# Reciprocal square roots of the norms on VectorE instead of GpSimd, and one set of SBUF offsets for both feed-forward blocks

## The chip, the core and the metric

The kernel runs on one core of one Trainium2 chip. The metric is device time in microseconds (us) of one execution, taken as the median of several runs of the same program. The engines are PE (TensorE), DVE (VectorE), ACT (ScalarE), POOL (GpSimd) and SP (SyncE, which here only starts DMAs).

## The reference

Two transformer blocks run one after the other on 256 tokens of width 1024. The first has a mixer (mLSTM and sliding-window attention), a cross attention to a memory, and a PEER layer over 16384 experts. The second has an even mixer (stick-breaking attention and retention), a convolutional feed-forward layer (`ffn0`), an odd mixer (gated linear attention) and a second feed-forward layer (`ffn1`). Each of these layers begins with a root-mean-square norm, and the first block ends with one:

```python
def rms_norm(x, g):
    xf = x.astype(jnp.float32)
    y = xf * lax.rsqrt(jnp.mean(xf * xf, axis=-1, keepdims=True) + EPS)
    return (y * g.astype(jnp.float32)).astype(x.dtype)

def conv_ffn(hn, w_up, conv_w, conv_b, w_down):
    u, v = jnp.split(hn @ w_up, 2, axis=-1)
    up = jnp.pad(u, ((0, 0), (CONV_WIDTH - 1, 0), (0, 0)))
    uc = conv_b + conv_w[0] * up[:, 0:s]
    for j in range(1, CONV_WIDTH):
        uc = uc + conv_w[j] * up[:, j:j + s]
    return (jax.nn.silu(uc) * v) @ w_down
```

Inside the even and odd mixers the same norm is also taken per head (of q, k and of the outputs).

## The kernel before

The activation `h` lies in SBUF with the 1024 features on 128 partitions in 8 tiles of 256 tokens. Every large product is made of three matmuls in a reduced float format: the operand is split into a high and a low part, and hi*hi, hi*lo and lo*hi are added up in PSUM. For weights, `weight` reads a piece of 512 KB over SP into `raw`; ACT writes `hi` (L430), DVE subtracts it and writes `lo` (L431). Five sets of raw, hi and lo buffers rotate up to the PEER layer and six after it, so a new piece can be split only when PE has done with an older one. L440 to L442 and L582 to L584 are the three matmuls, of 256 or 512 columns.

`Norm` splits the unnormalized `h` times the gain into `xh` and `xl` and lets the projection start on them; the reciprocal root is applied when the projection's result is taken from PSUM. It is made meanwhile: ACT and DVE square and add, PE sums over the partitions with a matmul against a column of ones (L200), `rsqrt` (L451 to L474) works on a tile of 128x2, and `spread` (L213 and L215) turns it into a row, `xR` or `uR`, by two matmuls against an identity and an ACT copy. Evacuations that need the row are queued until it is there. In program order the root is written after the first piece of the projection, the row after the third.

`rsqrt` has twelve operations: `rs_m` on DVE (L454) and eleven on POOL (a first guess from the bits, a refined `rs_z`, one more step to `rs_y` at L473). The chain stands alone: each operation needs the one before. `Final`, the norm between the two blocks, does two such roots in a row with three small products on POOL between and behind (L297, L298, L300), since it applies two norms at once. `head_norm` (L1349 to L1355) does the roots per head, with `rs_m` on POOL as well. `ev_o` in the mixer of the first block makes a negated copy `nr` on POOL.

The order in which instructions stand on each engine is not the order of the code. A scheduler lays them out by its own costs and by the buffers and pieces of work that are free; each engine then runs its list strictly in order.

Places in SBUF come from pools, in the order in which the pools are opened. `skip` (L397) takes some bytes and so moves all that follows in its pool; `off` moves a norm's tiles within their slot (`placed`). Before, the norm of `ffn1` has `off=16` elements and `ffn1` skips 32 bytes, where the other norms have 0 and `ffn0` skips 96. In the built program `xh` and `xl` begin at bytes 191552 and 199872 of a partition for the norms of even, ffn0 and odd, and at 191616 and 199936 for ffn1; `uh` and `ul`, the feed-forward layer's operands of the down product, begin at 119872 and 126016 in ffn0 and at 119808 and 125952 in ffn1.

## Time and profile before

| what | us |
|---|---|
| median of three runs | 1731.04 |
| lowest and highest of them | 1727.76 and 1736.29 |
| the profiled execution, its own time | 1739.33 |
| its span, first to last instruction | 1737.6 |
| PE busy in the span | 1683.0 |
| DVE, ACT, POOL busy | 1241.1, 873.8, 89.1 |

The profiled execution was 8.3 us above the median. A wait in the view of waits is time in which an engine had nothing to run, put down to what ended it. A row of the timeline is one instruction (or several alike): its start, its length, the engine, the line, what it writes and reads, and in brackets how long the engine was idle before it and what released it. [...] Matmuls overlap in the pipeline, so one is shown as longer than the distance between the starts of two.

### The profile page before, as it was taken

What the parts mean: (1) busy time and instruction counts of PE and PEld (TensorE: products, weight loads), DVE (VectorE), ACT (ScalarE), POOL (GpSimd) and SP (SyncE); (2) the same over time, 40 slices, a digit from 0 to 9 for tenths busy, and PEclk for the clock granted to TensorE, in tenths of its full rate; (3) what the DMA queues carried; (4) which work ended last, traced back from release to release, by engine and by line L of the source; (5) the groups of instructions that cost most, each with busy time, mean ns of one, the idle gap of its engine ahead of it and who ended that gap; (6) DMA issues with size and microseconds to landing.
All of it is one profiled execution on the core that took longest, in us unless ns stands there. A gap on an engine that the chain in (4) does not pass through costs nothing.

```text
span 1737.6 us, 33082 instructions
## 1 busy us (share of the span) xinstructions
PE 1683.0 (97%) x13220; PEld 1602.0 (92%) x13220; DVE 1241.1 (71%) x2309; ACT 873.8 (50%) x1358; POOL 89.1 (5%) x246
## 2 busy tenths in 40 slices
PE   7999999999999999999999999899999999999999
PEld 6879889999999999989999999678999987799998
DVE  6686559998798985678555556686777765677775
ACT  6445345545455554444444446464555454455543
POOL 1011010000000000000000000401100010210000
PEclk9999999999999999999999999999999999999999
DMA  7434454577555655889655556443455544345551
GB/s 263 152 104 147 146 172 131 187 236 260 175 186 199 194 196 188 309 289 299 190 189 186 185 189 210 157 135 110 162 192 186 191 159 155 102 162 190 188 188 62
DMA packets 97516, 318.03 MB, mean 183 GB/s; under 512 B 11841, under 2 KB 13505, under 8 KB 96850
## 3 DMA queue, kind: packets, MB, share of 16 engines
q1 hardware_dynamic: 89154, 301.39, 53.1%
q10 hardware_dynamic: 8208, 14.52, 2.2%
q8 instruction: 104, 1.70, 0.4%
q14 instruction: 50, 0.41, 0.1%
HBM read 299.36 MB, written 16.52 MB: 182 GB/s over the span
## 4 chain that ended last, share of the span: by engine, by line
PE 70%; DVE 7%; DMA 3%; POOL 2%; issue 2%; ACT 1%; SPq 0%; POOLq 0%; DVEq 0%; ACTq 0%
PE tp L440 11%; PE tp L441 11%; PE tp L442 11%; PE acc L582 8%; PE acc L583 8%; PE acc L584 8%; PE acc L440 3%; PE acc L441 3%; DMA u<-store 3%; PE acc L442 3%; DVE lo L431 2%; PE tp L1192 1%; PE tp L1193 1%; DVE ga L1244 1%; DVE w L1345 1%
## 5 line engine op out<-in xcount | busy, mean ns | idle before, releaser
L430 ACT ACTIVATE hi<-raw 128x1024 fp32r<-128x1024 f32 (+1 forms) x533 | 560.2, 1057 | 660.8 <-PE tp L441 246.6
L431 DVE TENSOR_TENSOR lo<-raw,hi 128x1024 fp32r<-128x1024 f32 (+1 forms) x533 | 646.7, 1219 | 309.5 <-ACT hi L430 309.2
L440 PE MATMUL tp<-xh,hi 128*128 128x256 f32 x1680 | 476.7, 284 | 0.6 <-ACT u L1207 0.6
L441 PE MATMUL tp<-xl,hi 128*128 128x256 f32 x1680 | 471.8, 281 | 0.0
L442 PE MATMUL tp<-xh,lo 128*128 128x256 f32 x1680 | 471.1, 280 | 0.6 <-DVE lo L431 0.6
L442 PEld LDWEIGHTS tp<-xh,lo 128*128 128x128 f32 x1680 | 317.1, 189 | 0.8 <-DVE lo L431 0.8
L440 PEld LDWEIGHTS tp<-xh,hi 128*128 128x128 f32 x1680 | 317.0, 189 | 0.8 <-ACT u L1207 0.8
L441 PEld LDWEIGHTS tp<-xl,hi 128*128 128x128 f32 x1680 | 317.2, 189 | 0.0
L583 PE MATMUL acc<-u,hi 128*128 128x256 f32 x1024 | 288.4, 282 | 5.6 <-DVE u L436 5.6
L584 PE MATMUL acc<-u,lo 128*128 128x256 f32 x1024 | 288.2, 281 | 1.4 <-DVE lo L431 1.4
L582 PE MATMUL acc<-u,hi 128*128 128x256 f32 x1024 | 287.9, 281 | 0.0
L583 PEld LDWEIGHTS acc<-u,hi 128*128 128x128 f32 x1024 | 193.0, 188 | 6.4 <-DVE u L436 6.4
L584 PEld LDWEIGHTS acc<-u,lo 128*128 128x128 f32 x1024 | 196.9, 192 | 1.8 <-DVE lo L431 1.8
L582 PEld LDWEIGHTS acc<-u,hi 128*128 128x128 f32 x1024 | 193.0, 189 | 0.0
L440 PE MATMUL acc<-hi,xh 128*128 128x512 f32 (+1 forms) x256 | 103.5, 406 | 1.6 <-ACT y L479 1.6
L441 PE MATMUL acc<-lo,xh 128*128 128x512 f32 (+1 forms) x256 | 101.7, 397 | 0.5 <-DVE lo L431 0.5
L442 PE MATMUL acc<-hi,xl 128*128 128x512 f32 (+1 forms) x256 | 101.1, 395 | 0.0
L582 PE MATMUL acc<-uh,hi 128*128 128x256 f32 x352 | 98.3, 280 | 0.1
L583 PE MATMUL acc<-ul,hi 128*128 128x256 f32 x352 | 98.1, 279 | 0.0
L584 PE MATMUL acc<-uh,lo 128*128 128x256 f32 x352 | 98.1, 279 | 0.0
L457 POOL TENSOR_SCALAR rs_g<-rs_m 128x2 int32<-128x2 int32 (+2 forms) x20 | 10.2, 510 | 1263.8 <-DVE fq L296 810.3
L582 PE MATMUL acc<-oh,hi 128*128 128x256 f32 x256 | 73.1, 285 | 0.0
(436 smaller groups left out, 2801.8 us busy)
## 6 DMA issues: line engine op xcount, KB each, us to landing
raw<-down SPq DMA_DIRECT2D x128, 512.0 KB, 3.7
raw<-up SPq DMA_DIRECT2D x128, 512.0 KB, 4.4
raw<-ffn_up SPq DMA_DIRECT2D x88, 512.0 KB, 3.5
raw<-ffn_down SPq DMA_DIRECT2D x44, 512.0 KB, 3.4
raw<-even_in SPq DMA_DIRECT2D x28, 512.0 KB, 4.4
store<-u ACTq DMA_DIRECT2D x55, 256.0 KB, 3.4
u<-store SPq DMA_DIRECT2D x55, 256.0 KB, 4.7
raw<-odd_in SPq DMA_DIRECT2D x24, 512.0 KB, 3.5
```

The source lines that it names most:

```text
L430: nc.scalar.activation(hi[:, c], raw[:, c], AF.Copy)
L431: nc.vector.tensor_sub(lo[:, c], raw[:, c], hi[:, c].bitcast(F32))
L440: mm(out, lh, rh, start=start, stop=False)
L441: mm(out, lh, rl, start=False, stop=False)
L442: mm(out, ll, rh, start=False, stop=stop)
L582: mm(out, wh[:, cs], oh, start=start and j == 0, stop=False)
L583: mm(out, wh[:, cs], ol, start=False, stop=False)
L584: mm(out, wl[:, cs], oh, start=False, stop=stop and j == 1)
L1192: mm(o, p1[:, b, :, e], hi[:, b, :, e], start=True, stop=False)
L1193: mm(o, p1[:, b, :, e], lo[:, b, :, e], start=False, stop=True)
L1244: nc.vector.tensor_mul(src, src, a)
L1345: nc.vector.match_replace(out=w, in_to_replace=val[:, :8], in_values=s, imm_value=-3e38)
```

## The change

All of `rsqrt` runs on DVE, in ten operations: a multiplication and an addition, or two multiplications, are fused into one (`scalar_tensor_tensor`) at three places. `Final`'s small products and `nr` run on DVE too. POOL keeps nothing of the roots. Behind the norms, `off` is 0 everywhere and both feed-forward layers skip 96 bytes. The tile `rs_b` falls away; the new pool `gaps` takes its 64 bytes.

```diff
-        nc.vector.tensor_copy(q, ps[:, 2:4])
-        nc.gpsimd.tensor_mul(q, q, self.rf)
-        nc.gpsimd.tensor_mul(q, q, self.rf)
-        r = b.rsqrt(q, 2, 1.0, keep=self.tag, e=nc.gpsimd)
-        nc.gpsimd.tensor_mul(r, r, self.rf)
+        nc.vector.tensor_mul(q, ps[:, 2:4], self.rf)
+        nc.vector.tensor_mul(q, q, self.rf)
+        r = b.rsqrt(q, 2, 1.0, keep=self.tag)
+        nc.vector.tensor_mul(r, r, self.rf)
...
-        e = self.nc.gpsimd
-        e.tensor_scalar(gi, ms.bitcast(I32), -0.5, float(0x5F1FFFF9), op0=ALU.mult, op1=ALU.add)
+        v.tensor_scalar(gi, ms.bitcast(I32), -0.5, float(0x5F1FFFF9), op0=ALU.mult, op1=ALU.add)
-        e.tensor_mul(a, y, y)
-        e.tensor_mul(a, a, ms)
-        e.tensor_scalar(a, a, -0.703952253, 0.703952253 * 2.38924456, op0=ALU.mult, op1=ALU.add)
+        v.tensor_mul(a, y, y)
+        v.scalar_tensor_tensor(a, a, -0.703952253, ms, op0=ALU.mult, op1=ALU.mult)
-        e.tensor_mul(z, y, a)
-        a = sp.tile([P, n], F32, tag="rs_b", name="rs_b")
-        e.tensor_mul(a, z, z)
-        e.tensor_mul(a, a, ms)
+        v.scalar_tensor_tensor(z, a, 0.703952253 * 2.38924456, y, op0=ALU.add, op1=ALU.mult)
+        v.tensor_mul(a, z, z)
+        v.tensor_mul(a, a, ms)
-        e.tensor_scalar(p, a, 0.375, -1.25, op0=ALU.mult, op1=ALU.add)
-        e.tensor_mul(p, p, a)
-        e.tensor_scalar(p, p, 1.875, None, op0=ALU.add)
+        v.scalar_tensor_tensor(p, a, -10.0 / 3.0, a, op0=ALU.add, op1=ALU.mult)
+        v.tensor_scalar(p, p, 0.375, 1.875, op0=ALU.mult, op1=ALU.add)
-        e.tensor_mul(out, p, z)
+        v.tensor_mul(out, p, z)
...
-            return lambda: Norm(self, self.h, i, self.xq, off=16 if i == 8 else 0)
+            return lambda: Norm(self, self.h, i, self.xq, off=0)
...
+            self.skip(self.pool(ctx, "gaps"), 64)
...
-                nc.gpsimd.tensor_scalar(nr, x.r[t], -1.0, None, op0=ALU.mult)
+                nc.vector.tensor_scalar(nr, x.r[t], -1.0, None, op0=ALU.mult)
...
-            self.skip(mp, 32 if l else 96)
+            self.skip(mp, 96)
```

In the built program the ten operations do not stand together. On DVE around the norm of ffn0 there stood before, with `lo` the low half of a weight piece, `rs_m` the first operation of the root and `w` the first evacuation that needs `xR`:

```order
L454 TENSOR_SCALAR rs_m_14523<-tp_14520 128x2
L431 TENSOR_TENSOR lo_14634<-raw_14631,hi_14633 128x1024
L431 TENSOR_TENSOR lo_14673<-raw_14670,hi_14672 128x1024
L431 TENSOR_TENSOR lo_14713<-raw_14710,hi_14712 128x1024
L431 TENSOR_TENSOR lo_14747<-raw_14744,hi_14746 128x1024
L431 TENSOR_TENSOR lo_14778<-raw_14775,hi_14777 128x1024
L1538 TENSOR_TENSOR w_14612<-acc_14495,xR_14607 128x256
```

On the same engine at the same place there stands now (lines of the changed file; its `lo` is L430):

```order
L453 TENSOR_SCALAR rs_m_14488<-tp_14485 128x2
L430 TENSOR_TENSOR lo_14596<-raw_14593,hi_14595 128x1024
L455 TENSOR_SCALAR rs_g_14490<-rs_m_14488 128x2
L430 TENSOR_TENSOR lo_14635<-raw_14632,hi_14634 128x1024
L458 TENSOR_TENSOR rs_a_14492<-rs_g_14490 128x2
L430 TENSOR_TENSOR lo_14675<-raw_14672,hi_14674 128x1024
L459 SCALAR_TENSOR_TENSOR rs_a_14492<-rs_a_14492,rs_m_14488 128x2
L430 TENSOR_TENSOR lo_14709<-raw_14706,hi_14708 128x1024
L461 SCALAR_TENSOR_TENSOR rs_z_14495<-rs_a_14492,rs_g_14490 128x2
L430 TENSOR_TENSOR lo_14740<-raw_14737,hi_14739 128x1024
L462 TENSOR_TENSOR rs_a_14492<-rs_z_14495 128x2
L430 TENSOR_TENSOR lo_14780<-raw_14777,hi_14779 128x1024
```

Each step of the root is now followed by a `lo`, six in all, of which the sixth stood behind `w` before; the last four steps follow without one.

On PE around the row of the odd mixer's norm there stood before, with `xR`'s matmul at L213 between the last product of one weight piece and the first of the next:

```order
L441 MATMUL acc_16944<-lo_16966,xh_16758 128x512
L442 MATMUL acc_16944<-hi_16965,xl_16759 128x512
L213 MATMUL tp_16982<-ident_87,rs_y_16941 128x128 x2
L440 MATMUL acc_16943<-hi_16997,xh_16758 128x512
L441 MATMUL acc_16943<-lo_16998,xh_16758 128x512
```

On PE there stands at that place now:

```order
L439 MATMUL acc_16903<-hi_16956,xh_16720 128x512
L440 MATMUL acc_16903<-lo_16957,xh_16720 128x512
L213 MATMUL tp_16941<-ident_92,rs_y_16900 128x128 x2
L441 MATMUL acc_16903<-hi_16956,xl_16721 128x512
L439 MATMUL acc_16902<-hi_16978,xh_16720 128x512
```

L213 moved behind eleven of the next piece's twelve matmuls. In the same way it moved behind 21 matmuls of 128x256 in the first mixer, 22 in the cross attention, and behind 13 of those and five smaller ones in the PEER queries; in the memory's norm, the even mixer and both feed-forward layers it stayed.

On DVE in `Final` of the even mixer there stood before, with the rest of both roots on POOL and `y` the evacuation that waits for them:

```order
L454 TENSOR_SCALAR rs_m<-tp 128x2
L296 COPY fq<-tp 128x2
L431 TENSOR_TENSOR lo<-raw,hi 128x1024 x4
L481 TENSOR_SCALAR y<-acc,rs_y 128x512
L431 TENSOR_TENSOR lo<-raw,hi 128x1024
```

On DVE there stands now, from the end of the first root (ahead of it eight `lo` stand between its steps):

```order
L468 TENSOR_TENSOR rs_y_13176<-rs_p_13173,rs_z_13169 128x2
L296 TENSOR_TENSOR fq_13178<-tp_13157,rs_y_13176 128x2
L297 TENSOR_TENSOR fq_13178<-fq_13178,rs_y_13176 128x2
L453 TENSOR_SCALAR rs_m_13181<-fq_13178 128x2
L455 TENSOR_SCALAR rs_g_13183<-rs_m_13181 128x2
L430 TENSOR_TENSOR lo_13506<-raw_13503,hi_13505 128x1024
L458 TENSOR_TENSOR rs_a_13185<-rs_g_13183 128x2
L307 SCALAR_TENSOR_TENSOR h_8918<-h_8918,g_89,fR_13336 128x256
L459 SCALAR_TENSOR_TENSOR rs_a_13185<-rs_a_13185,rs_m_13181 128x2
```

All eight residual operations `h` (L307), which stood much later before, now stand between the second root's steps, so `y` stands behind nine `lo` and eight `h`.

Of the offsets, in the built program all norms from even on have `xh` at 191808 and `xl` at 200000, and ffn1 has `uh` and `ul` where ffn0 has them. The weight buffers keep their addresses.

## Rows read from the trace of the kernel before

**Rows 1.** The page's first part: busy us, share of the span, instructions.

```profile
PE 1683.0 (97%) x13220; PEld 1602.0 (92%) x13220; DVE 1241.1 (71%) x2309; ACT 873.8 (50%) x1358; POOL 89.1 (5%) x246
```

**Rows 2.** Waits of PE: what it waited for, us in total, times, longest.

```profile
PE tp L213 <- POOL rs_y L473: 19.3, 7, 3.3
...
PE tp L1383 <- DVE y L1377: 5.9, 2, 5.4
...
PE tp L599 <- DVE ro L1503: 2.7, 1, 2.7
```

**Rows 3.** Timeline of PE at the norm of ffn0.

```profile
1231.10 0.28 PE L442 MATMUL acc<-xh,lo 128*128 128x256 f32 x1
1234.22 0.71 PE L213 MATMUL tp<-ident,rs_y 128*128 128x128 f32 x4 [2.85 <-POOL rs_y L473]
```

**Rows 4.** Timeline of POOL at the same place: fifth and sixth of eleven operations.

```profile
1231.42 1.05 POOL L464 TENSOR_TENSOR rs_z<-rs_g,rs_a 128x2 f32<-128x2 f32 x1
1232.55 0.19 POOL L466 TENSOR_TENSOR rs_b<-rs_z 128x2 f32<-128x2 f32 x1
```

**Rows 5.** Timeline of DVE at the same place.

```profile
1226.59 0.15 DVE L454 TENSOR_SCALAR rs_m<-tp 128x2 f32<-128x2 f32 x1
1226.66 5.75 DVE L431 TENSOR_TENSOR lo<-raw,hi 128x1024 fp32r<-128x1024 f32 x5
```

**Rows 6.** Timeline of ACT at the same place: the sixth weight piece.

```profile
1231.30 1.06 ACT L430 ACTIVATE hi<-raw 128x1024 fp32r<-128x1024 f32 x1 [1.25 <-DVE lo L431]
```

**Rows 7.** Timeline of DVE in the first mixer: two small operations, the second needing the first.

```profile
81.01 0.17 DVE L880 TENSOR_TENSOR ss<-ss,rc 128x8 f32<-128x8 f32 x1
81.21 0.17 DVE L881 TENSOR_TENSOR ss<-ss,rc 128x8 f32<-128x8 f32 x1
```

**Rows 8.** Windows after two waits of PE: length, busy us by engine, PEclk, DMA share, GB/s.

```profile
105.70:109.10 3.40, 3.29 (x21) 2.46 (x22) 2.17 (x8) 2.09 (x7) 0.00 (x0) 1.00 0.58 223
...
1234.80:1238.20 3.40, 3.40 (x19) 3.40 (x18) 2.81 (x6) 1.48 (x3) 0.00 (x0) 0.50 0.64 251
```

**Rows 9.** Timeline of PE at the norm of the odd mixer.

```profile
1421.47 0.40 PE L441 MATMUL acc<-lo,xh 128*128 128x512 f32 x1
1421.71 0.40 PE L442 MATMUL acc<-hi,xl 128*128 128x512 f32 x1
1425.02 0.71 PE L213 MATMUL tp<-ident,rs_y 128*128 128x128 f32 x4 [2.91 <-POOL rs_y L473]
```

**Rows 10.** Timeline of PE at the memory's norm.

```profile
105.74 0.71 PE L213 MATMUL tp<-ident,rs_y 128*128 128x128 f32 x4 [1.19 <-POOL rs_y L473]
```

**Rows 11.** Timeline of PE in the even mixer, at `Final`.

```profile
1097.53 0.51 PE L440 MATMUL acc<-hi,xh 128*128 128x512 f32 x1 [1.62 <-ACT y L479]
...
1105.99 1.11 PE L1383 MATMUL tp<-ident,y 128*128 128x128 f32 x4 [5.40 <-DVE y L1377]
```

**Rows 12.** Timeline of DVE at the same place.

```profile
1085.81 0.16 DVE L454 TENSOR_SCALAR rs_m<-tp 128x2 f32<-128x2 f32 x1 [1.14 <-PE tp L200]
```

**Rows 13.** Instructions of line 308: engine, operation, count, ns (least, median, most).

```profile
L308 DVE SCALAR_TENSOR_TENSOR h<-h,g,fR x8: 470/477/478, 1113.6 to 1130.4; 128x256 f32<-128x256 f32 x8
```

**Rows 14.** Timeline of DVE at the output norm of the retention.

```profile
1196.83 0.67 DVE L1354 TENSOR_REDUCE rn1s<-rn1q 128x4 f32<-128x512 f32 x1
1198.34 1.23 DVE L431 TENSOR_TENSOR lo<-raw,hi 128x1024 fp32r<-128x1024 f32 x1 [0.84 <-ACT hi L430]
1202.48 1.14 DVE L1503 SCALAR_TENSOR_TENSOR ro<-ro,rs_y,gate 128x128 f32<-128x128 f32 x4 [2.92 <-POOL rs_y L473]
```

**Rows 15.** Windows in the PEER layer, in ffn0 and in ffn1; first busy us and count: PE.

```profile
789.00:801.00 12.00, 12.00 (x109) 12.00 (x108) 9.60 (x12) 5.59 (x7) 0.00 (x0) 1.00 0.96 325
809.00:1071.00 262.00, 262.00 (x2227) 262.00 (x2226) 145.60 (x150) 121.38 (x140) 0.00 (x0) 1.00 0.62 197
1240.00:1405.00 165.00, 164.87 (x1417) 164.68 (x1417) 121.80 (x185) 85.37 (x123) 0.00 (x0) 1.00 0.57 186
1560.00:1725.00 165.00, 165.00 (x1401) 165.00 (x1400) 117.69 (x178) 81.17 (x117) 0.00 (x0) 1.00 0.50 162
```

More of the change, by code (lines that the diff above doesn't have):

```diff
@@ L449, in copy, with rsqrt @@
             self.nc.vector.tensor_copy(out, in_)
-    def rsqrt(self, ss, n, inv, keep=None, e=None):
-        sp = self.sp
+    def rsqrt(self, ss, n, inv, keep=None):
+        sp, v = self.sp, self.nc.vector
         ms = sp.tile([P, n], F32, tag="rs_m", name="rs_m")
-        (e or self.nc.vector).tensor_scalar(ms, ss, inv, EPS, op0=ALU.mult, op1=ALU.add)
-        e = self.nc.gpsimd
+        v.tensor_scalar(ms, ss, inv, EPS, op0=ALU.mult, op1=ALU.add)
         gi = sp.tile([P, n], I32, tag="rs_g", name="rs_g")
-        e.tensor_scalar(gi, ms.bitcast(I32), -0.5, float(0x5F1FFFF9), op0=ALU.mult, op1=ALU.add)
+        v.tensor_scalar(gi, ms.bitcast(I32), -0.5, float(0x5F1FFFF9), op0=ALU.mult, op1=ALU.add)
         y = gi.bitcast(F32)
         a = sp.tile([P, n], F32, tag="rs_a", name="rs_a")
-        e.tensor_mul(a, y, y)
-        e.tensor_mul(a, a, ms)
-        e.tensor_scalar(a, a, -0.703952253, 0.703952253 * 2.38924456, op0=ALU.mult, op1=ALU.add)
+        v.tensor_mul(a, y, y)
+        v.scalar_tensor_tensor(a, a, -0.703952253, ms, op0=ALU.mult, op1=ALU.mult)
         z = sp.tile([P, n], F32, tag="rs_z", name="rs_z")
-        e.tensor_mul(z, y, a)
-        a = sp.tile([P, n], F32, tag="rs_b", name="rs_b")
-        e.tensor_mul(a, z, z)
-        e.tensor_mul(a, a, ms)
+        v.scalar_tensor_tensor(z, a, 0.703952253 * 2.38924456, y, op0=ALU.add, op1=ALU.mult)
+        v.tensor_mul(a, z, z)
+        v.tensor_mul(a, a, ms)
         p = sp.tile([P, n], F32, tag="rs_p", name="rs_p")
-        e.tensor_scalar(p, a, 0.375, -1.25, op0=ALU.mult, op1=ALU.add)
-        e.tensor_mul(p, p, a)
-        e.tensor_scalar(p, p, 1.875, None, op0=ALU.add)
+        v.scalar_tensor_tensor(p, a, -10.0 / 3.0, a, op0=ALU.add, op1=ALU.mult)
+        v.tensor_scalar(p, p, 0.375, 1.875, op0=ALU.mult, op1=ALU.add)
         out = sp.tile([P, n], F32, tag="rk_" + keep if keep else "rs_y", name="rs_y")
-        e.tensor_mul(out, p, z)
+        v.tensor_mul(out, p, z)
         return out
@@ L1354, in head_norm @@
         nc.vector.tensor_reduce(ss, sq, axis=AX.X, op=ALU.add)
-        return self.rsqrt(ss, n, 1.0 / d, keep=tag, e=nc.gpsimd)
+        return self.rsqrt(ss, n, 1.0 / d, keep=tag)
     def even(self, x, nxt):
```

## The prediction

> **What bounds the kernel now.** The page's first part comes first: PE is busy 97% of the span, DVE 71%, POOL 5% [rows 1]. What PE loses is 1737.6 - 1683.0 = 54.6 us of idle time and whatever it runs at a lower clock. Second, the view of waits says for what PE stood idle: 19.3 us, in seven waits, for POOL's last step of a root (`rs_y`) at L213 [rows 2]. Third, one of them is read in the timelines, at ffn0. PE starts its last free matmul at 1231.10 and goes on at 1234.22 with the matmul that spreads the root [rows 3]. On POOL the fifth step of the chain takes 1.05 us and the sixth 0.19 us [rows 4], though they are alike in size. What changed between them is DVE: it ran five `lo` in a row from 1226.66 to 1232.41 [rows 5]. So the chain is slow because a POOL step beside a `lo` takes as long as that `lo`, about 5.75/5 = 1.15 us; alone, eleven steps of 0.19 us would be 2.1 us of work.
>
> Fourth, the clock. In the 3.4 us after ffn0's wait of 2.85 us PEclk is 0.50; after the memory's wait of 1.19 us it stays 1.00 [rows 8, 10]. A stretch of 3.4 us at half clock does the work of 1.7, so a wait near 3 us costs 1.7 us more than its length.
>
> **The chain on DVE, step by step.** It is not put on a free engine: between its steps the order has a `lo` each, and DVE runs them strictly in order. In a queue a small operation takes its place in 1226.66 - 1226.59 = 0.07 us [rows 5]; where it needs the one before, 81.21 - 81.01 = 0.20 us [rows 7]. At ffn0 that is six `lo` of 1.15 us and six small steps among them, then four dependent steps. From 1226.59 the first five `lo` and six small steps end at 1226.59 + 5.75 + 6 x 0.07 = 1232.8; the sixth `lo` has its `hi` from 1232.36 [rows 6] and ends at 1233.9; four steps of 0.20 bring `rs_y` to 1234.7. L213 stood at 1234.22 with POOL; it is not moved there, so PE waits **0.6 us longer**, between 0 and +1.4 (all steps at 0.20). ffn1 is built alike: 1.2 us together, bounds 0 and 2.8.
>
> Where the gain comes from is PE's own order. At **four norms** (first mixer, cross attention, PEER queries, odd mixer) L213 now stands behind more matmuls. That is 21 or 22 of 128x256 at 165/1417 = 0.116 us [rows 15], or 2.5 us; eleven of 128x512 at 1421.71 - 1421.47 = 0.24 us [rows 9], or 2.6 us; in the PEER queries 13 and five smaller ones, some 2.0 us if the small ones are priced alike. The mean is 2.4 us. The chain itself is as long as before, since five or six `lo` stand in it on either engine, so the wait of (19.3 - 1.2)/6 = 3.0 us [rows 2, 10] falls to 0.6. With more work done ahead, PE comes sooner to a PSUM bank that only the queued evacuations free; this costs between nothing and one more length of L213's group, 0.71 us [rows 3]; no row shows it, and I take 0.3, nearer to nothing since L213's own length is only part of that way. Saved: 4 x (2.4 - 0.3) = **8.4 us**, bounds 6.7 and 9.6.
>
> The **memory's norm** keeps L213's place, and its chain now has `lo`s and two other evacuations between. Its wait of 1.19 us [rows 10] becomes 2.5 by the same count as at ffn0, with one more `lo` than there beside POOL: +1.3, bounds 0 and +3.
>
> **Final** gets longer. From `rs_m` at 1085.81 [rows 12]: eight `lo`, 9.2 us, ten steps of which four dependent, 0.6 + 0.8; `fq` and the next two, 0.8; a ninth `lo`, 1.15; eight residuals of 0.48 [rows 13] less the overlap of 0.07, 3.3; the steps among and behind them, 1.0: `y` starts at 1102.6. PE's next matmul followed `y` by some 0.7 us at 1097.53 [rows 11]; it moves to 1103.3, 5.8 later. But twelve matmuls on, PE waited once more, until 1105.99, for the q heads' norm [rows 11], two roots on POOL. At the **retention** two such roots take from the end of the last sum, 1197.50, to 1202.48 for the first [rows 14], 5.0 us; on DVE the two stand in pairs, 20 steps of 0.07 to 0.20, 1.4 to 4.0 us, of which I take 2.0 (ten dependent distances, the partner in their shadow), plus the `lo` at 1198.34, 1.15 or more. So `ro` starts 1.5 us sooner there and the wait of 2.7 us [rows 2] falls to 1.2: **-1.5**, bounds 0 and -2.7. At the q heads the pair saves 3.0 and the `lo` that stood among them 0.8 more: 5.8 - 3.8 = **+2.0**, bounds 0 and +5.8.
>
> The other roots (k heads, odd outputs) and `nr` have no wait in rows 2 and lie beside PE's matmuls: nothing. If that cover were gone, each would cost its chain of 2.0 us.
>
> Waits together: -8.4 - 1.5 + 1.2 + 1.3 + 2.0 = **-5.4 us**.
>
> **The clock.** Five waits (the four and the retention's) fall below 1.2 us, and after one of 1.19 PEclk stayed at 1.00 [rows 8]. Each gives 1.7 us back; as one of the four may meet a second wait at the PSUM bank just behind, I count four: **-6.8**, bounds -8.5 and 0. Of the memory's 2.5 us no row tells; it lies between 1.19 and 2.85, and I count nothing and keep +1.7 as a bound. Both ffn and the even mixer keep their half-clock stretches.
>
> **The offsets.** In equal stretches PE ran 1417 matmuls in ffn0 and 1401 in ffn1 [rows 15]: 0.1164 against 0.1178 us each. ffn1 gets ffn0's offsets for `uh` and `ul`, and the same `xh` and `xl`. If the pace hangs on these, its some 180 us at 1.1% give **-2.0**. But PEER speaks against a pace by offsets alone: on one set of buffers it had 109 matmuls in 12 us (three of them begun before, so 0.113 each) and then 2227 in 262 us, 0.1177 [rows 15]. So both layers could settle at 0.113, -4.9 and -7.1 (1540 matmuls each), or both at 0.1178, +2.1 and 0. I take -2.0, the pace that the same operands have in ffn0; bounds -12.0 and +2.1. [...]
>
> **Sum.** -5.4 - 6.8 - 2.0 = -14.2 us. The profiled execution would take 1739.3 - 14.2 = 1725.1. It was itself 8.3 above the median of the runs, so against that the forecast is 1731.0 - 14.2 = **1716.8 us**.
>
> **The rivals.**
> A: both feed-forward layers settle at 0.113: ten more, 1707. For it: PEER's first stretch and the rest of the offsets being equal; against: it lasted only 12 us there.
> B: half the clock and no offsets: -5.4 - 3.4 = -8.8, 1722. [...]
> C: the moved L213 finds the root later by as much as it was moved, because DVE, in order, holds the small steps behind `lo`s that wait for ACT. Waits are then what they were: +4.5 - 1.5 - 2.0, about 1.0 up, 1732. For it: DVE idled for `hi` [rows 14]; against: at ffn0 the five `lo` ran without a gap.
> D, slower: the weight buffers. A `lo` needs its `hi`, which needs a buffer that PE must free; in ffn0 the sixth `hi` waited 1.25 us [rows 6]. Where a step of the root stands behind such a `lo` and PE in turn stands at L213, the chain is late by more than PE's matmuls cover. It decides from about 2.4 us at the four norms. Then they save nothing, the feed-forward layers take 2.8, the memory 3.0 and its clock 1.7, `Final` 5.8, the retention gives 1.5, offsets and the clock nothing: +11.8, 1743. Against it: in the order every such `lo` belongs to a piece whose `hi` was already under way.
> That the change doesn't do what it says can be left out, as POOL's steps are gone from the order.
>
> **How the numbers follow.** Forecast 0.50 (by its bounds between 1709 and 1722), A 0.10, B 0.17, C 0.13, D 0.10. The range leaves out D and the far half of A: 1703 to 1735. What a measurement can tell from no change is about 0.5%, 8.7 us: below 1722.4 is faster (forecast, A and a small part of B, 0.63), above 1739.7 slower (D and a little of C, 0.11), between them 0.26.
>
> **What would show it.** Right: PE's waits at L213 fall from 19.3 to about 9 us, now for DVE, and lie in the memory's norm and both feed-forward layers; four or five stretches at 0.50 are gone; PE's wait for `y` at L1379 (L1383 before) ends about 2 us later after `rs_m`; ffn1 shows some 1417 matmuls in 165 us. Wrong: waits of 3 us at L213 in the four norms (C, D), idle DVE between the steps of a root (D), a stretch at 0.50 behind the memory's norm, or a pace of 0.1178 in ffn0.

## The result and the profile after

| | before | after |
|---|---|---|
| median of four runs, us | 1732.87 | 1705.72 |
| lowest and highest | 1727.76 to 1736.29 | 1700.60 to 1709.04 |
| the profiled execution, its own time | 1739.33 | 1709.04 |
| its span | 1737.6 | 1707.3 |

The ratio of after to before is 0.984, with a 95% interval of 0.981 to 0.987: faster by 27 us. The forecast was 14.2 us faster and 1716.8 us; the range, 1703 to 1735, holds the measured 1705.7, but near its edge. So about half of the gain was not in the sum.

The page's first part of the kernel after stands against [rows 1]: busy us, share of the span, instructions.

```profile
PE 1662.3 (97%) x13220; PEld 1582.3 (93%) x13220; DVE 1262.0 (74%) x2504; ACT 874.4 (51%) x1358; POOL 0.8 (0%) x11
```

PE has the same 13220 matmuls, but is busy for 20.7 us less. Its idle time, 1707.3 - 1662.3 = 45.0 us, fell by 9.6. So two thirds of the 30.3 us between the spans are not waits that went away; they are matmuls that ran quicker. The waits of PE answer to [rows 2]: us in total, times, longest.

```profile
PE tp L213 <- DVE rs_y L468: 8.5, 5, 3.3
...
PE acc L439 <- ACT y L474: 5.8, 1, 5.8
...
PE tp L213 <- DVE mx L912: 2.5, 1, 2.5
```

The waits at L213 are 11.0 us in six instead of 19.3 in seven. The one put down to `mx` is the memory's norm; there `rs_y` is the operation just ahead of `mx` on DVE, started at 104.75 and ended at 104.89:

```profile
104.75 0.14 DVE L468 TENSOR_TENSOR rs_y<-rs_p,rs_z 128x2 f32<-128x2 f32 x1
```

The retention's wait of 2.7 us at L599 has no row any more. The long wait of the even mixer stands at another matmul (L439 instead of L1383). The timeline of PE shows where the rest lies: first mixer, memory, cross attention (two rows), ffn0, odd mixer; start, length, and in brackets the idle time before.

```profile
24.70 0.60 PE L213 MATMUL tp<-ident,rs_y 128*128 128x128 f32 x4
...
105.04 1.19 PE L213 MATMUL tp<-ident,rs_y 128*128 128x128 f32 x4 [2.50 <-DVE mx L912]
...
178.31 0.71 PE L213 MATMUL tp<-ident,rs_y 128*128 128x128 f32 x4 [0.88 <-DVE rs_y L468]
...
179.95 1.99 PE L1019 MATMUL tp<-kT,q 128*128 128x256 f32 x8 [0.70 <-DVE q L1060]
...
1219.69 0.71 PE L213 MATMUL tp<-ident,rs_y 128*128 128x128 f32 x4 [3.25 <-DVE rs_y L468]
...
1405.62 0.61 PE L213 MATMUL tp<-ident,rs_y 128*128 128x128 f32 x4
```

Two of the four moved rows have no wait at all. The cross attention has 0.88 us and, just behind it, 0.70 at L1019: the second wait that the prediction had priced between 0 and 0.71. The windows view shows the clock behind the memory's norm, behind the cross attention's row and at two places of the even mixer, then the PEER layer, ffn0 and ffn1 in stretches of the length of [rows 15]: length, PE busy and its matmuls, the other engines, PEclk (the clock granted to PE, as a share of its full clock: 0.50 is half clock), DMA share, GB/s.

```profile
105.00:108.50 3.50, 3.46 (x10) 2.41 (x11) 2.08 (x9) 1.92 (x7) 0.00 (x0) 0.50 0.62 193
178.40:181.80 3.40, 2.70 (x15) 2.29 (x16) 2.33 (x5) 1.33 (x2) 0.00 (x0) 1.00 0.92 352
1094.40:1097.60 3.20, 3.20 (x8) 2.52 (x9) 2.63 (x17) 1.06 (x2) 0.00 (x0) 0.50 0.00 0
1099.00:1105.00 6.00, 6.00 (x31) 5.02 (x32) 5.71 (x15) 3.85 (x5) 0.00 (x0) 1.00 0.27 91
802.00:1045.00 243.00, 243.00 (x2066) 243.00 (x2065) 136.51 (x139) 113.90 (x130) 0.00 (x0) 1.00 0.60 196
1225.00:1390.00 165.00, 164.86 (x1453) 164.62 (x1452) 123.37 (x187) 86.93 (x126) 0.00 (x0) 1.00 0.59 189
1533.00:1698.00 165.00, 165.00 (x1456) 164.89 (x1455) 120.54 (x183) 83.11 (x120) 0.00 (x0) 1.00 0.51 164
```

Behind 0.88 us the clock stayed at 1.00; behind the memory's 2.50 it was at 0.50. And ffn0 and ffn1 have 1453 and 1456 matmuls in 165 us where they had 1417 and 1401 [rows 15]; the clock was 1.00 on both sides, so this is not the clock.

PE has the same matmuls on both sides, in the same order but for the moved rows and some swaps of neighbours inside the mixers, the memory, the cross attention and the retention (230 of 13188 places). So, where the two orders agree, the start of the n-th matmul in the one trace can be taken from that in the other. The difference grows by this much in each stretch (us; minus is earlier in the kernel after; a small part that comes back right behind is added in):

| stretch | measured | predicted |
|---|---|---|
| first mixer's norm | -1.4 | |
| cross attention's norm | -3.0 | |
| PEER queries' norm | -5.2 | |
| odd mixer's norm | -5.2 | |
| retention | -4.1 | |
| these five together | -18.9 | -16.7 |
| memory's norm | +3.1 | +1.3 |
| both feed-forward norms | +1.8 | +1.2 |
| `Final` in the even mixer | -2.7 | +2.0 |
| ffn0 and ffn1 behind their norms | -11.8 | -2.0 |
| the rest, most of it in the PEER layer | -1.7 | 0 |
| all | -30.2 | -14.2 |

The prediction gave the clock 6.8 us in one sum; here it stands with the five stretches that it counted it for. Two terms carry the miss: the offsets, by 9.8 us, and `Final`, by 4.7.

The rest is a sum of parts that partly cancel. About 2 us of it is a pace again: in PEER's first large product PE ran more matmuls in 30 us of the kernel after (second row) than of the kernel before (first row), at the same clock:

```profile
405.00:435.00 30.00, 30.00 (x257) 30.00 (x257) 30.00 (x75) 16.04 (x25) 0.00 (x0) 1.00 0.67 223
```
```profile
405.00:435.00 30.00, 30.00 (x267) 30.00 (x267) 30.00 (x61) 14.74 (x23) 0.00 (x0) 1.00 0.70 221
```

This is no effect of the change: the kernel after, profiled twice more, has 257 there both times.

### The profile page after: what moved, and what is told of

The parts are those of the page before. It is cut to its first block, busy times and chain, and to the rows that moved or that the text cites. A ratio compares the mean times of both kernels' runs of the same rounds, so it can differ in the third digit from the quotient of the medians.

```text
span 1707.3 us, 33027 instructions
## 1 busy us (share of the span) xinstructions
PE 1662.3 (97%) x13220; PEld 1582.3 (93%) x13220; DVE 1262.0 (74%) x2504; ACT 874.4 (51%) x1358; POOL 0.8 (0%) x11
## 4 chain that ended last, share of the span: by engine, by line
PE 83%; DVE 10%; DMA 4%; issue 2%; ACT 1%; SPq 0%; ACTq 0%; DVEq 0%
PE tp L439 11%; PE tp L441 11%; PE tp L440 11%; PE acc L578 10%; PE acc L579 9%; PE acc L577 9%; PE acc L439 5%; PE acc L440 5%; PE acc L441 5%; DVE lo L430 3%; DMA u<-store 2%; PE tp L1188 1%; PE tp L1189 1%; DMA raw<-w_in_t 1%; ACT hi L429 1%
## 5 line engine op out<-in xcount | busy, mean ns | idle before, releaser
L430 DVE TENSOR_TENSOR lo<-raw,hi 128x1024 fp32r<-128x1024 f32 (+1 forms) x533 | 649.0, 1220 | 295.1 <-ACT hi L429 294.8
L439 PE MATMUL tp<-xh,hi 128*128 128x256 f32 x1680 | 473.2, 282 | 0.4 <-ACT u L1203 0.4
L439 PEld LDWEIGHTS tp<-xh,hi 128*128 128x128 f32 x1680 | 316.8, 189 | 0.6 <-ACT u L1203 0.6
L579 PEld LDWEIGHTS acc<-u,lo 128*128 128x128 f32 x1024 | 192.7, 188 | 2.9 <-DVE lo L430 2.9
L439 PE MATMUL acc<-hi,xh 128*128 128x512 f32 (+1 forms) x256 | 101.3, 398 | 6.4 <-ACT y L474 5.8
L578 PE MATMUL acc<-ol,hi 128*128 128x256 f32 x256 | 71.8, 280 | 0.0
```

The lines of the kernel that those rows point to most:

```text
L430: nc.vector.tensor_sub(lo[:, c], raw[:, c], hi[:, c].bitcast(F32))
L439: mm(out, lh, rh, start=start, stop=False)
L578: mm(out, wh[:, cs], ol, start=False, stop=False)
L579: mm(out, wl[:, cs], oh, start=False, stop=stop and j == 1)
```

## Experiments

Lines in the rows are those of each kernel's own file; L213 and its like is the matmul that spreads the root. The pace of a stretch below is the mean distance between the starts of neighbouring matmuls of 256 columns. Places of operands are given modulo 256 bytes; that 256 is the period that counts was not tested.

### The roots alone

```diff
-            return lambda: Norm(self, self.h, i, self.xq, off=0)
+            return lambda: Norm(self, self.h, i, self.xq, off=16 if i == 8 else 0)
...
-            self.skip(mp, 96)
+            self.skip(mp, 32 if l else 96)
```

> The changed kernel with the old offsets (16 elements for the last norm, 32 and 96 bytes in the two feed-forward layers); only the roots run on VectorE. If the offsets set the pace of the feed-forward layers and the two halves of the change add up: both layers run at their old paces (some 1417 matmuls in 165 us in ffn0, 1401 in ffn1), PE's order and waits at L213 are those of the changed kernel, and the time lies 18 us under the kernel before, near 1715. If the pace is drawn by chance after each wait and the offsets do nothing: at least one layer shows 1456 in 165 us, and the time is near 1706 to 1711.

Measured: 1716.95 us, 0.992 of the kernel before (0.989 to 0.994). The waits of PE are those of the kernel after, and the matmuls in 165 us of ffn0 are no more than before:

```profile
PE tp L213 <- DVE rs_y L468: 7.6, 5, 3.3
```
```profile
1223.00:1388.00 165.00, 165.00 (x1404) 165.00 (x1403) 119.23 (x179) 84.53 (x120) 0.00 (x0) 1.00 0.57 184
```

So the roots bring about 13 us by the medians (1729.98 - 1716.95). The table's rows for norms, retention and `Final` add up to -16.7, within the interval of -11 to -19.

### The offsets alone

The edit is made on the kernel before:

```diff
-            return lambda: Norm(self, self.h, i, self.xq, off=16 if i == 8 else 0)
+            return lambda: Norm(self, self.h, i, self.xq, off=0)
...
-            self.skip(mp, 32 if l else 96)
+            self.skip(mp, 96)
```

> The kernel before with the new offsets alone; the roots stay on GpSimd. If the offsets set the pace: both feed-forward layers run a matmul each 0.113 us (some 1456 in 165 us), waits for rs_y at L213 stay at 19.3 us in seven, and the time is 12 us under the kernel before, near 1721. If the pace is drawn by chance: 1417 and 1401 matmuls or any other pair, and no reason for a gain, near 1733. My forecast's own term (ffn1 gets ffn0's pace and ffn0 keeps its own) would give 1417 in both and 2 us.

Measured: 1720.89 us, 0.995 (0.993 to 0.997). The roots' waits are as in [rows 2], and the windows of ffn0 and ffn1 differ from each other:

```profile
PE tp L213 <- POOL rs_y L473: 19.5, 7, 3.2
```
```profile
1230.00:1395.00 165.00, 164.86 (x1452) 164.62 (x1452) 124.97 (x192) 87.50 (x127) 0.00 (x0) 1.00 0.58 190
1540.00:1705.00 165.00, 165.00 (x1403) 165.00 (x1402) 120.04 (x184) 83.31 (x121) 0.00 (x0) 1.00 0.51 166
```

The offsets alone bring 9 us by the medians; with the roots' 13 that is 22 of the 27 (by the ratios 9.2 + 14.7 = 23.9, and the whole has an interval of 22 to 34). But ffn0 took the short pace here and ffn1 did not, with the same places of their operands. That fits neither "the operands set the pace" nor "they don't matter".

### Half of the old offsets each

```diff
-            self.skip(mp, 96)
+            self.skip(mp, 32 if l else 96)
```

> The changed kernel with the second feed-forward layer's u, uh and ul back at their old offset (0 instead of 64 modulo 256). If each product's pace hangs on its own operands: ffn1's up products stay at 0.1133 us, its 528 down products go to 0.118, and the layer takes 2.5 us more than in the changed kernel. If the layer has one pace as a whole: 1401 matmuls in 165 us, 7.4 us more. If offsets do nothing: 1456 in 165 us as in the changed kernel.

```diff
-            return lambda: Norm(self, self.h, i, self.xq, off=0)
+            return lambda: Norm(self, self.h, i, self.xq, off=16 if i == 8 else 0)
```

> The changed kernel with the last norm's offset of 16 elements back, which makes the slots of xh and xl 128 bytes longer: xl lies at 192 modulo 256 against xh at 64 in ffn0 (at 0 against 128 in ffn1), as before; uh and ul stay. If each product's pace hangs on its own operands: in both layers the up products, 1056 each, go to 0.1177 us and the down products stay at 0.1133; 1417 matmuls in 165 us in both, some 9.3 us more than the changed kernel. If offsets do nothing: 1456 in 165 us in both.

Measured, one profiled execution each: 1710.40 and 1713.56 us. First the window of ffn1 in the kernel with the old `skip`, then those of ffn0 and ffn1 in that with the old `off`:

```profile
1530.00:1695.00 165.00, 165.00 (x1416) 164.98 (x1415) 119.14 (x180) 82.27 (x118) 0.00 (x0) 1.00 0.50 163
```
```profile
1220.00:1385.00 165.00, 165.00 (x1403) 165.00 (x1402) 119.45 (x180) 83.27 (x117) 0.00 (x0) 1.00 0.56 186
1533.00:1698.00 165.00, 165.00 (x1419) 165.00 (x1419) 119.60 (x181) 82.94 (x119) 0.00 (x0) 1.00 0.50 163
```

`skip` moves `uh` and `ul` in ffn1 alone (with the layer's other tiles in that pool), and the pace of its down part went to 118.75 ns. But the up part, whose operands stayed, went to 115.60 too, between the two paces: a product's own operands are not all that counts. `off` for one norm changed ffn0 as well. The addresses give a reason: with an `off` anywhere the slot of `xh` and `xl` is wider for all norms from the even mixer on, so `xl` lies at 199872 and not 200000, and `xh` 256 bytes lower. Modulo 256 bytes `xh` is at 64 and `xl` at 192 in ffn0, 128 and 0 in ffn1; without `off` both are at 64 in both layers.

### The same program again

The kernel after, unchanged.

> The changed kernel itself, a second profiled execution. If a stretch's pace belongs to the program (its offsets and order): each stretch shows the pace that it had, 0.1133 us in both feed-forward layers and 0.1178 in the PEER up products. If it is drawn in each execution among those that the offsets allow: at least one of the stretches with equal offsets (PEER up, feed-forward, the products out of the mixers) shows the other pace, and the time moves by that, up to 10 us.

Measured: 1718.82 us, ten more than the first profiled execution. The window of ffn0:

```profile
1228.00:1393.00 165.00, 165.00 (x1404) 165.00 (x1403) 119.28 (x180) 84.52 (x120) 0.00 (x0) 1.00 0.56 183
```

The same program had 1453 there the first time. So the pace is not fixed by the program: the up part of ffn0 ran at 113.33 ns in the one execution and at 117.77 in the other.

### Both operands at 128

```diff
+        off = 16 if i >= 5 else 0
...
-        t = pool.tile([P, 8 * T + 32], dtype, tag=tag, name=tag)
+        t = pool.tile([P, 8 * T + 64], dtype, tag=tag, name=tag)
```

> The changed kernel with xh and xl of the second block both at 128 modulo 256 (where the weights' hi and lo lie) instead of both at 64. If only the distance between xh and xl counts: the up products of both feed-forward layers run at 0.1133 or at an even 0.1178 as with 64. If the place against the weights counts: they run at another pace or in another pattern, and the down products keep theirs.

Measured: 1712.88 us in one execution. `xh` and `xl` both lie at 128 modulo 256. The window of ffn0:

```profile
1218.00:1383.00 165.00, 165.00 (x1402) 165.00 (x1402) 119.38 (x179) 83.31 (x117) 0.00 (x0) 1.00 0.57 186
```

The up parts ran at 119.6 ns, longer than with any other place. That `xh` and `xl` lie alike modulo 256 is therefore not enough. The edit also widened their slots, so that `xl` lies 8448 bytes behind `xh` where the other kernels have 8192 or 8320; which of the two did it was not tested. The paces of all profiled executions, in ns (PEER up is that layer's second large product, from about 810 us on):

| kernel | PEER up | ffn0 up, down | ffn1 up, down |
|---|---|---|---|
| before | 117.78 | 117.68, 113.65 | 117.80, 118.30 |
| after | 117.78 | 113.33, 113.38 | 113.33, 113.34 |
| after again | 117.78 | 117.77, 117.73 | 113.33, 113.33 |
| after, timed again | 117.78 | 113.33, 113.38 | 113.33, 113.34 |
| roots alone | 117.78 | 117.83, 117.60 | 117.79, 118.30 |
| offsets alone | 113.33 | 113.33, 113.45 | 117.77, 117.79 |
| old `skip` | 117.78 | 113.33, 113.37 | 115.60, 118.75 |
| old `off` | 113.33 | 117.82, 117.61 | 117.84, 113.48 |
| both at 128 | 113.33 | 119.63, 114.21 | 119.61, 114.13 |
| unfused | 117.78 | 113.33, 113.39 | 113.33, 113.34 |
| root first | 113.33 | 113.33, 113.37 | 117.77, 117.79 |
| root first in ffn | 113.33 | 117.77, 117.75 | 113.33, 113.33 |
| rows put back | 117.78 | 113.33, 113.38 | 113.33, 113.33 |
| residuals behind | 113.33 | 113.33, 113.36 | 113.33, 113.33 |

With `xh`, `xl`, `uh` and `ul` all at 64, 15 of 19 layers ran at the short pace from end to end and 4 at the long one. With `xl` at another place than `xh` all six up parts were long. With `uh` and `ul` at 0 all three down parts were at 118.3 or more. The operands of PEER up lie at the same places in every kernel, at 64, and it too had the short pace in 6 of 14. It was long both in the kernel before and in the profile after, so this draw is no part of the 30.2 us; in a single comparison it can make up to 9.4 (some 2120 matmuls by 4.45 ns).

### The root unfused, on VectorE

```diff
-        v.scalar_tensor_tensor(a, a, -0.703952253, ms, op0=ALU.mult, op1=ALU.mult)
+        v.tensor_mul(a, a, ms)
+        v.tensor_scalar(a, a, -0.703952253, 0.703952253 * 2.38924456, op0=ALU.mult, op1=ALU.add)
...
-        v.scalar_tensor_tensor(z, a, 0.703952253 * 2.38924456, y, op0=ALU.add, op1=ALU.mult)
+        v.tensor_mul(z, y, a)
...
-        v.scalar_tensor_tensor(p, a, -10.0 / 3.0, a, op0=ALU.add, op1=ALU.mult)
-        v.tensor_scalar(p, p, 0.375, 1.875, op0=ALU.mult, op1=ALU.add)
+        v.tensor_scalar(p, a, 0.375, -1.25, op0=ALU.mult, op1=ALU.add)
+        v.tensor_mul(p, p, a)
+        v.tensor_scalar(p, p, 1.875, None, op0=ALU.add)
```

> The changed kernel with the twelve unfused operations of before, all on VectorE; new offsets. If the gain comes from the engine and from where PE's order puts L213, not from the shorter chain: L213 stands within a few matmuls of where the changed kernel has it, the four moved waits stay under 1 us, and the time is within 4 us of the changed kernel (two more lo slots in a chain, up to 2.3 us, where L213 isn't moved: ffn0, ffn1, memory). If the fusing is what counts: the four waits return to near 3 us with their half-clock stretches, some 15 us over the changed kernel, near 1721.

Measured: 1714.63 us, 0.990 (0.985 to 0.995). The waits of PE:

```profile
PE tp L213 <- DVE rs_y L470: 12.5, 7, 3.8
```

The four moved norms wait for 0.63, 0.36, 0.39 us and not at all, with L213 another 2 to 10 matmuls further back in PE's order; ffn0 and ffn1 wait for 3.65 and 3.84, about half a us more than with ten operations, the memory 2.9 and the even mixer 6.3. By the n-th matmul it ends 8.1 us later than the kernel after: 2.6 by the end of the cross attention, 2.0 more by 470 us, 1.2 in the rest of the PEER layer, 1.1 at `Final` and 1.2 from there on, most of it at the two feed-forward norms. The 2.0 are the pace in PEER's first product (257 matmuls from 405 to 435 us, not 267) and no effect of the edit; the 1.2 in the rest of PEER were not followed. So most of the gain at the norms is there without the fusing: it comes from the other engine and the order that goes with it, while fusing gives some 4 to 5 us on top (2.6 + 1.1 + 1.2).

### The rows put back where they were

`L213` is set back to its place on PE of the kernel before in the first mixer, cross attention and odd mixer, and to eight matmuls behind it in the PEER queries; the roots still run on DVE.

```diff
+        self.fixed = i in (0, 2, 3, 7)
...
+        if self.fixed:
+            b.row, b.behind = m.ins, 48
...
+        with ExitStack() as ctx:
+            if self.behind:
+                self.behind -= 1
+                ctx.enter_context(self.tc.issue_after(self.row))
```

> The changed kernel with L213 put back, at the four norms where it had moved, behind the third weight piece as in the kernel before (PE rows 74, 955, 1403 and 11179); the roots and the DVE order stay. If the place in PE's order is what gained there: the four waits come back, near 3 us each, with 3.4 us or more at half clock behind each, and the time rises by 10 to 16 us over the changed kernel. If the engine itself had made the root earlier: the waits stay under 1 us and the time within 3 us.

Measured: 1715.80 us, 0.988 (0.984 to 0.993). Its waits, and two of the four in PE's timeline (the others are 1.15 in the first mixer and 2.09 in the PEER queries):

```profile
PE tp L214 <- DVE rs_y L476: 15.3, 7, 3.3
```
```profile
178.77 0.58 PE L214 MATMUL tp<-ident,rs_y 128*128 128x128 f32 x1 [3.06 <-DVE rs_y L476]
...
1411.58 0.49 PE L214 MATMUL tp<-ident,rs_y 128*128 128x128 f32 x2 [2.10 <-DVE rs_y L476]
```

By the n-th matmul the four stretches cost 2.6 + 3.2 + 2.9 + 2.5 = 11.2 us against the kernel after, out of the 14.8 that they had gained. So the place of the row in PE's list is three quarters of that gain. The waits come back as 2.1 us on the mean, not 3.1 as in the kernel before (2.92, 3.29, 3.23 and 2.91). From `rs_m` to the end of `rs_y` DVE needs less than POOL in the first mixer (5.0 us for 5.9) and the odd mixer (7.0 for 7.8), and about as much in the other two; in the PEER queries the eight matmuls cover 0.9 us.

### The root ahead of the queued `lo`

```diff
+        self.b.ahead, self.b.delayed = self.b.root, 6
...
+        b.ahead, b.delayed = nc.vector.tensor_mul(r, r, self.rf).ins, 9
...
+            if self.delayed:
+                self.delayed -= 1
+                ctx.enter_context(self.tc.issue_after(self.ahead))
```

> The changed kernel in which the lo of the next six weight pieces (nine at Final) may only be issued behind the root, so that DVE runs the ten operations without a lo between. If the lo between the steps is what is left of the cost: the root takes 2.0 us from rs_m to rs_y instead of 8, the waits of 3.3 us at L213 in both feed-forward layers, of 2.5 at the memory and of 5.8 at Final go or fall under 1.5 with their half-clock stretches, and the time falls by 12 to 20 us under the changed kernel, to 1686 to 1694. If the lo are needed as early as they stand: PE then waits for lo instead, 2 us at each of the eight norms, and the time stays within 4 us of the changed kernel or rises.

Measured: 1719.99 us, 0.993 (0.991 to 0.996), slower than the kernel after. DVE's timeline at ffn0 shows the first and last operation of a root with nothing between its steps, 1.94 us from `rs_m`'s start to the end of `rs_y`:

```profile
1215.72 0.16 DVE L458 TENSOR_SCALAR rs_m<-tp 128x2 f32<-128x2 f32 x1 [0.70 <-PE tp L200]
...
1217.50 0.16 DVE L473 TENSOR_TENSOR rs_y<-rs_p,rs_z 128x2 f32<-128x2 f32 x1
```

But PE did not get by. Its waits for roots still come to 10.9 us, and one for a held `lo` is new in the memory's stretch:

```profile
PE tp L214 <- DVE rs_y L473: 10.9, 7, 2.0
```
```profile
102.41 0.58 PE L446 MATMUL acc<-uh,lo 128*128 128x256 f32 x1 [6.84 <-DVE lo L435]
```

The scheduler answered the shorter root by moving the row up to right behind the sums, so PE again stood at it; and it waited 6.84 and, at `Final`, 3.60 us for low halves that now came late. So the interleaved `lo` are not a plain loss.

### The same in both feed-forward layers only

The row is held at its place here, behind the third piece, and only ffn0 and ffn1 take the root ahead.

```diff
+        self.ahead = i in (6, 8)
...
+        if self.ahead:
+            self.b.ahead, self.b.delayed = self.b.root, 6
...
+            if self.ahead:
+                ctx.enter_context(self.b.tc.issue_after(self.b.lastmm))
             self.R = self.spread(self.r2, self.tag + "R")
```

> The changed kernel in which, at the two feed-forward norms alone, the next six lo may only be issued behind the root and L213 only behind the third weight piece, where it stands now. If the lo between the steps are what PE waits for there: the root is ready 2.0 us after rs_m, before PE comes to L213, both waits of 3.3 us and their half-clock stretches go, and the time falls by 8 to 10 us, to about 1697 to 1700 on the scale of the changed kernel's 1705.7 to 1709. If the lo held back are needed at once: PE waits at L441 for lo instead, 2 to 3 us at each of the two, and the time stays within 3 us. The pace of each stretch can move it by up to 10 us either way and is read apart.

Measured: 1710.04 us, 0.985 (0.982 to 0.989), which the kernel after (0.984) does not differ from. PE's timeline at ffn0, then DVE's:

```profile
1199.75 0.38 PE L451 MATMUL acc<-xh,lo 128*128 128x256 f32 x1 [3.16 <-DVE lo L440]
```
```profile
1196.62 0.16 DVE L463 TENSOR_SCALAR rs_m<-tp 128x2 f32<-128x2 f32 x1 [0.70 <-PE tp L201]
...
1198.40 0.16 DVE L478 TENSOR_TENSOR rs_y<-rs_p,rs_z 128x2 f32<-128x2 f32 x1
1198.47 8.03 DVE L440 TENSOR_TENSOR lo<-raw,hi 128x1024 fp32r<-128x1024 f32 x7
```

The root is done 1.9 us after `rs_m`, the wait of 3.25 us at the row is gone, and one of 3.16 stands at the next piece's `lo`. ffn1 has a wait of 3.16 us for a `lo` as well. So, in this order at least, PE waits for DVE's work on root and `lo` together, and moving the root ahead only changes which of them it waits for.

### `Final`'s residuals behind the q heads

```diff
+        with self.b.tc.issue_after(self.b.heads):
             self.b.nc.vector.scalar_tensor_tensor(self.h[:, k], self.h[:, k], self.f[:, k:k + 1], self.R,
...
-                    nc.vector.tensor_mul(y, y, r[:, :, None].to_broadcast([P, 8, 64]))
+                    scaled = nc.vector.tensor_mul(y, y, r[:, :, None].to_broadcast([P, 8, 64]))
+                    if which == 0:
+                        self.heads = scaled.ins
```

> The changed kernel with the eight residual products of Final (L307) held back behind the q heads' norm, so that they no longer stand between the second root's steps. If they are part of what PE waits for there, as I priced them: y starts 3 us sooner after rs_m (15.9 us in the changed kernel), PE's wait of 5.8 us falls to 2.8 to 3.3, the half-clock stretch behind it stays or goes, and the even mixer's start is 3 to 5 us shorter; the whole falls by as much. If the q heads' norm ends last there whatever y does: PE's wait before y falls and the wait before L1379 grows by as much, and the even mixer's start takes as long as now.

The kernel after ran beside it on the same chip, unchanged:

> The changed kernel itself, timed again beside the last variant on the same chip, with a third profiled execution. If the pace of each stretch is drawn in each execution: its times spread over some 10 us or more, its median lies between 1705 and 1716, and the profile shows yet another set of paces in PEER up and the feed-forward layers; waits at L213 and the order's effects are those of the first profile within 1 us. If a pace belongs to the program: the times agree within 0.3% and the profile repeats one of the two sets seen.

Measured: 1699.61 us, 0.982 (0.978 to 0.985), and the kernel after 1708.67, 0.986 (0.982 to 0.989). DVE at `Final`, then PE:

```profile
1065.07 0.16 DVE L454 TENSOR_SCALAR rs_m<-tp 128x2 f32<-128x2 f32 x1 [1.06 <-PE tp L200]
...
1078.95 0.75 DVE L477 TENSOR_SCALAR y<-acc,rs_y 128x512 f32<-128x512 f32 x1
```
```profile
1079.69 0.50 PE L440 MATMUL acc<-hi,xh 128*128 128x512 f32 x1 [3.84 <-ACT y L475]
```

From `rs_m` to `y` it takes 13.9 us, with the residuals between the steps 15.9, and PE's wait is 3.84 instead of 5.84. By the n-th matmul the even mixer gains 2.4 us. This is the best median of all kernels, but of the 9 us between the two only these 2.4 are explained by the edit; in the two profiles another 9 come from the PEER layer, which here ran at 113.33 ns. Whether the median has a part of that draw stays open, as single executions other than the profiled one leave no trace. The kernel after, timed again, showed the paces of its first profile in PEER up and in both feed-forward layers, but not in PEER's first product, and its five times spread over 7.3 us; neither of the two cases set down for it came out whole.

## Why the prediction was right, and where not

**What bounds the kernel, and the four moved norms: right.** PE stood at L213 because the root came late, and behind more matmuls it waits less: 0, 0.88 and 0.70, 0.76, and 0 us where 0.6 + 0.3 each was predicted. That the place on PE is the cause was only read from the order; the rows put back show it, with 11.2 of 14.8 us. One step of it was off in part: the chain was to be "as long as before". From `rs_m` to the end of `rs_y` it took 5.03, 9.00, 8.66 and 6.99 us where it had taken 5.92, 8.82, 8.70 and 7.82, so it is shorter by 0.9 and 0.8 in the two mixers and about the same in the other two.

**Both feed-forward norms: right.** At ffn0 the chain from `rs_m` to the start of `rs_y` took 7.8 us; six `lo` and ten small steps had been counted to 8.1. DVE's rows answer to [rows 5]:

```profile
1211.66 0.15 DVE L453 TENSOR_SCALAR rs_m<-tp 128x2 f32<-128x2 f32 x1
1211.73 1.21 DVE L430 TENSOR_TENSOR lo<-raw,hi 128x1024 fp32r<-128x1024 f32 x1
...
1219.47 0.16 DVE L468 TENSOR_TENSOR rs_y<-rs_p,rs_z 128x2 f32<-128x2 f32 x1
```

Waits went from 2.85 to 3.25 us [rows 3]; predicted was +0.6. Rivals C and D fall: the four norms had no waits near 3 us, and DVE did not stand idle between the steps.

**The clock: right where it was counted, not at all places.** The five stretches at half clock went where the waits fell below 1.2 us, as forecast: to 0, 0.88, 0.76 and 0 us at the four norms and to none at the retention. The memory's norm had its wait sized well (2.50 us), but its clock was counted at nothing: +3.1 in place of +1.3, about the bound of +1.7. Behind 1.19 us of wait PEclk had been 1.00 there [rows 8]; behind 2.50 it is 0.50, from 104.3 to 111.1 us. The size is not fixed by the program: in the kernel after, timed again, the half clock ended after 3.4 us instead of 6.8 and the norm cost 1.5 us less. And a wait of 1.94 us in the PEER layer, at 747.46, left PEclk at 1.00.

**`Final`: the step that failed is "Both ffn and the even mixer keep their half-clock stretches", taken to mean that nothing changes there.** The even mixer did keep 6.8 us at half clock, but on other work. The wait steps were off by 1 us only: `y` 15.9 us after `rs_m` where 16.8 was predicted, and L1379 21.2 us after it where it had been 20.2, so +1.05 for +2.0. DVE and PE after, against [rows 11, 12]:

```profile
1077.71 0.16 DVE L453 TENSOR_SCALAR rs_m<-tp 128x2 f32<-128x2 f32 x1 [1.06 <-PE tp L200]
...
1093.59 0.75 DVE L476 TENSOR_SCALAR y<-acc,rs_y 128x512 f32<-128x512 f32 x1
```
```profile
1094.33 0.79 PE L439 MATMUL acc<-hi,xh 128*128 128x512 f32 x1 [5.84 <-ACT y L474]
...
1098.94 0.66 PE L1379 MATMUL tp<-ident,y 128*128 128x128 f32 x4
...
1102.20 0.60 PE L1379 MATMUL tp<-ident,y 128*128 128x128 f32 x4
```

What was missed is which of the two waits is the long one. Before, 1.62 us stood first and 5.40 last, and half clock lay behind the last, so every matmul in it delayed all that follows. Now 5.84 stands first, and half clock falls on most of the twelve matmuls up to 1098.94. They end about when the first of the q heads is ready, at 1098.19 + 1.29/2 = 1098.84, so their slowness is hidden in what had been the second wait:

```profile
1098.19 1.29 DVE L1373 TENSOR_TENSOR y<-y,rs_y 128x512 f32<-128x512 f32 x2
```

From one L1379 to the next PE takes 1102.20 - 1098.94 = 3.26 us; before, the same work from L1383 to L1383 ran at half clock:

```profile
1105.99 1.11 PE L1383 MATMUL tp<-ident,y 128*128 128x128 f32 x4 [5.40 <-DVE y L1377]
...
1112.00 0.38 PE L1383 MATMUL tp<-ident,y 128*128 128x128 f32 x2
```

That is 6.01 us, so 2.75 go, and +1.05 becomes -1.70. Another 1.0 of the -2.7 lies outside these two points and was not followed.

**The retention: right in sign, short in size.** `ro` starts 3.1 us after the last sum ends, where it was 5.0:

```profile
1186.06 0.68 DVE L1350 TENSOR_REDUCE rn1s<-rn1q 128x4 f32<-128x512 f32 x1
...
1189.86 0.35 DVE L1499 SCALAR_TENSOR_TENSOR ro<-ro,rs_y,gate 128x128 f32<-128x128 f32 x1
```

So the chain gave 1.9 us, not 1.5. PE's wait of 2.7 us is gone altogether, not cut to 1.2, since the matmul that reads `ro` also stands ten matmuls of 128x256 further back in PE's order, some 1.1 us, which the prediction did not see:

```profile
1190.27 0.33 PE L594 MATMUL tp<-ident,ro 128*128 128x128 f32 x1
```

With the clock behind it the retention gains 4.1 us, where 1.5 + 1.7 had been counted.

**The offsets: the step that failed is "the pace that the same operands have in ffn0".** Two things in it were wrong. ffn0's 0.1164 us was no pace but a mean of two, 117.7 ns in its up part and 113.7 in its down part. And ffn0's operands did not stay: modulo 256 its `xl` moved from 192 to 64, as the addresses said (in ffn1 `xh` moved from 128 and `xl` from 0 to 64). So both layers could settle at 113.3, and in the profiled execution did: 1024 up matmuls by 4.35 ns are 4.5 us in ffn0, and in ffn1 1024 by 4.47 and some 510 by 4.96 are 7.1. This was rival A, given 0.10 at 1707 us. Its ground, that PEER shows two paces on one set of buffers, was the right one; "against: it lasted only 12 us there" was not. What decides the draw stays open. The chip alone isn't it: the kernel after, run again, and the one with its rows put back ran on the same chip with the same places, and ffn0 had 117.77 ns in the one and 113.33 in the other. But those are two programs; that one program on one chip shows both paces is not shown, as no chip is known to have given two profiles of one program.

Rival B counted half the clock and nothing for the offsets. No run shows either term: all five stretches at 0.50 at the four norms and the retention are gone, and with the offsets alone the median fell by 9 us, of which it stays open how much was the draw. With places that differ by 64 bytes modulo 256 the pace of the down part went from 113.3 to 118.75 ns (old `skip`), and that of the up parts to 119.6 (both at 128, the distance changed too).

In sum, the roots came out as forecast within about 5 us, and 11.8 of the 30.2 us between the profiles hang on a pace in the feed-forward layers that the sum held for a small matter; about 2 more lie in PEER's first product. The range held, but the median of 1705.7 us lies outside the forecast's own bounds, 1709 to 1722, and next to rival A. That A's paces came up in both layers was partly luck: the same program also ran ffn0 at the long one, and that execution took 1718.82 us.

## What to carry to other kernels

When a chain of small steps moves to another engine, look first at where its reader stands in its own queue afterwards; here three quarters of the gain at four norms (11.2 of 14.8 us) came from matmuls that the scheduler put ahead of the reader, and the retention gained by the same. At the norms and the retention, before and after, PEclk was 0.50 behind each of the twelve waits of 2.50 to 5.84 us, in stretches of 3.4 or 6.8 us. At half the work that is some 1.7 or 3.4 us, an estimate, on top of the wait's length, unless it falls on work that would have waited anyway (2.75 us went so at `Final`), so it pays to see which of two waits is the last. And before a rate is carried from one stretch to another, split it by part and compare the addresses of all its operands, and run the same program twice: here ffn0 ran at 113.33 or at 117.77 ns in one program, whose two profiled executions of 1709.04 and 1718.82 us lie 9.8 us apart, more than the 9.1 us by which the offsets alone moved the median.

## What was not expected of the hardware

- Of the 70 stretches of 256-column matmuls in the table of paces, 62 ran on the mean at one of two paces, 113.3 to 113.7 or 117.6 to 117.8 ns from start to start, with PEclk at 1.00 in the windows shown, and kept it for hundreds of matmuls (PEER up in the kernel after: 2066 in 243 us). The same program showed both in ffn0 (1453 and 1404 matmuls in 165 us).
- In these 14 profiles the pace went with the places of the operands, given modulo 256 bytes: all at 64, 15 of 19 layers at 113.3 to 113.5 ns and 4 at 117.7 to 117.8; `xl` at another place than `xh`, all six up parts at 117.7 to 117.8; `xh` and `xl` at 128, 119.6; `uh` and `ul` at 0, 118.3 to 118.8.
- The ten dependent operations of a root, without others between, took 1.94 us on DVE at ffn0 (the root ahead of the queued `lo`), 0.20 from start to start as in [rows 7]. With six `lo` between they took 8.0 there (kernel after, 1211.66 to 1219.63).
